# Seven-product weight pairs in 24 instead of 13 projection chunks of an encoder layer, with the attention work spread over the steps on two PSUM banks

## The chip, the cores and the metric

One core of one Trainium2 chip. The metric is the device time of one execution in microseconds (us), the median of three runs; one further execution was recorded by the hardware profiler, and all shares, rows and durations below are that execution's.

## The reference, cut to what matters

```python
h = layer_norm(x)                        # x: 256 tokens x 4096
p = h @ w_in                             # 4096 x 13312: 26 chunks of 512 columns
# attention, 16 query heads, 4 key/value heads of 128:
s = q @ k.T * 128**-0.5 - slope_h * |t - s|      (only |t - s| <= 128)
a = softmax over keys and one sink logit per head of s;  y_attn = (a @ v) * silu(z)
# convolution branch, 2048 channels:
y_conv = c_b * conv3(c_c * c_h) * silu(c_z)
out = layer_norm(2**0.25 * h + concat(y_conv, y_attn) @ w_out)
```

All of it is float32.

## The kernel before, in words

**A product of two floats as three.** TensorE reads float32 operands in a fast, rounded form (`F32R`). So each operand is cut into a rounded part `hi` and a rest `lo`, and x·w is taken as xh·wh + xh·wl + xl·wh, three matmuls into one PSUM accumulator. The normalised input stands transposed in `xT` (32 tiles of 128 rows, kt 0 to 31; hi of the 256 tokens, then lo). The weights come from HBM in steps, and each is cut in the kernel: `split_hi` (L124) has ScalarE (ACT) copy the raw tile into `whi`, `split_lo` (L129) has VectorE (DVE) subtract that from the raw tile into `wlo`.

**Steps and chunks.** The 13312 columns of the projection are 26 chunks of 512, in the order K, V, then Z and Q of each of four head groups, then for each of four channel groups CC, CH, CZ, CB (`IN_ORDER`, L36). A chunk takes all 32 tiles of kt. A plain step (`s`) brings four tiles of kt (1 MB) and multiplies with 24 matmuls of 512 columns (`mm`, L157). A pair step (`S`) brings two tiles of kt (0.5 MB) and forms the same 256 x 512 part of the product in Strassen's way, in seven products of half width (`mm_pair`, L176): 21 matmuls of 256 columns in place of 12 of 512. For it DVE makes four further blocks from the raw weights (`sums`, L112), the cut covers seven blocks, and sums of x stand in `SC` (`x_sums`, L499). Three of the seven products go into the chunk's accumulators `acc`, four into two banks `pacc`, which `pair_sums` (L513) and `whole` (L524) add in when the chunk is over. Before, 13 chunks have six pairs and five plain steps each (the first CZ to the last CZ); the other 13 chunks are eight plain steps.

**The order of the work is written by hand.** The main loop (L637) goes over the steps j. It issues the matmuls of step j, then whatever `at(j, ...)` has put down for that step, then the loads of step j+6 (or 7), then `sums(j + 4)` and `split(j + 3)`. Each engine works through its instructions in that order. `whi` and `wlo` have three buffers, so the cut for step j+3 begins when TensorE (PE) has finished step j, and has to be done before PE gets to step j+3: two steps later.

**A head group.** When chunk Q of a group is over, `q_turn` transposes q on PE. For each of its four heads come `scores` (6 matmuls on PE, then on DVE the bias, the row maximum and its negative `nm`, on ACT two exponentials with row sums and the sink's `es`, on DVE the denominator, its reciprocal `rd` and the division of the probabilities p), `p_tr` (four transposes on PE, `pT` cut into hi on ACT and lo on DVE), and `pv` (6 matmuls on PE, the gate on DVE). They stand at steps 2 to 8 after Q (L631), on four PSUM banks `att`.

Of the kernel before, what the change touches and what calls it, by code (L numbers as in the profile page):

```python
# [40 lines left out]
NS = 6  # L41
HW = W // 2
HT = S // 2
S_FIRST = IN_ORDER.index(C_CZ)
S_LAST = len(IN_ORDER) - 2
S_UNITS = "s S s S S s S s S S s".split()


def units(ci):

    if not S_FIRST <= ci <= S_LAST:
        return [("in", ci, q) for q in range(NPC)]
    q, p, us = 2 * NS // PK, 0, []
    for u in S_UNITS:
        if u == "s":
            us.append(("in", ci, q))
            q += 1
        else:
            us.append(("pair", ci, p))
            p += 1  # L60
    assert q == NPC and p == NS
    return us
# [9 lines left out]
def encoder_kernel(ctx: ExitStack, tc: tile.TileContext, x, emb_g, emb_b, wi, ws, conv_w, sink, wo, ln_g, ln_b, out):  # L72
# [25 lines left out]
    raw, wh, wl = {}, {}, {}  # L98

    def load(j, to=None):  # L100
        if j >= len(steps):
            return
        kind, a, b = steps[j]
        if kind == "pair":
            to = raw[j] = pc.tile([P, PIECE], F32, name="praw", bufs=3)
            nc.sync.dma_start(out=to[:, 0:4 * HW], in_=ws[IN_PAIRS.index((a, b))])
        else:
            if to is None:
                to = raw[j] = wpool.tile([P, PIECE], F32, name="wraw")
# [64 lines left out]
    pacc, SC = {}, None  # L174

    def mm_pair(j):  # L176

        _, ci, p = steps[j]
        hi, lo = (t.pop(j).rearrange("p (b w) -> p b w", w=HW) for t in (wh, wl))
        if p == 0:  # L180
# [3 lines left out]
        x = lambda kt, i: (xT[:, kt, i * HT:(i + 1) * HT], xT[:, kt, S + i * HT:S + (i + 1) * HT])  # L184
        sc = lambda k: (SC[:, p, 0, k, :], SC[:, p, 1, k, :])
        p0, p1, c0, c1 = pacc[ci, 0], pacc[ci, 1], acc[ci, 0], acc[ci, 1]
        for (ah, al), w, o, opens, closes in (
                (x(a, 0), 2, p0[:, 0, :], True, False), (x(b, 0), 3, c0[:, 0:HW], False, False),
                (sc(3), 1, c0[:, HW:W], False, False), (x(b, 1), 7, c1[:, 0:HW], False, False),
                (sc(0), 5, p1[:, 1, :], True, False), (sc(1), 6, p0[:, 1, :], False, True),  # L190
                (sc(2), 4, p1[:, 0, :], False, True)):
            nc.tensor.matmul(o, ah, hi[:, w, :], start=(opens and p == 0), stop=False)  # L192
            nc.tensor.matmul(o, ah, lo[:, w, :], start=False, stop=False)  # L193
            nc.tensor.matmul(o, al, hi[:, w, :], start=False, stop=(closes and p == NS - 1))  # L194
# [174 lines left out]
    ph = ExitStack()  # L369
    pa = ph.enter_context(tc.tile_pool(name="pa", bufs=1))  # L370

    def build_tab():
# [3 lines left out]
        tf = pa.tile([P, 2, S], F32, name="tf", tag="p", bufs=3)  # L376
# [42 lines left out]
    def end_z(ci, g):  # L419
        st_["z"] = token_tile(pa, "z", ci, AF.Silu)  # L420

    def z_turn(g):
        zT = st_["zT"] = pa.tile([P, GROUP, S], F32, name="zT")
        for b, ps in enumerate(turned(st_.pop("z"))):
            nc.scalar.activation(zT[:, 2 * b:2 * b + 2, :], ps, AF.Copy)
# [445 lines left out]
```

## Time and profile before

| | |
|---|---|
| median of three runs | 1561.48 us (1560.03 to 1562.35) |
| the profiled execution | 1562.12 us, span of its instructions 1560.3 us |
| granted TensorE clock, mean | 0.996 |
| busy DVE / ACT | 1056.4 us (68%) / 680.6 us (44%) |
| moved by DMA | 312.84 MB, 200 GB/s over the span |

The page of the profile gives the busy time of each engine, the chain of work that ended last, and the costliest groups of instructions. A group's row has line, engine, operation, output tile <- input tiles, shapes, the count, then the summed busy time and the mean of one in ns, then the idle time just before. In the timeline a row is one instruction or several alike: start, length, engine, line; square brackets hold the idle time before it and what ended it. PE rows overlap, since matmuls are pipelined: the distance between two starts is what one costs.

### The profile page before, as it was taken

Reading aid. Unit: us, or ns where it says so; the run is one execution under the profiler, and the core shown is the slowest. Engines: PE = TensorE matmul, PEld = TensorE weight load, DVE = VectorE, ACT = ScalarE, POOL = GpSimd, SP = SyncE. Lnnn points to the kernel's source line nnn. Section 1 sums busy time; section 2 is a strip of 40 time slices with the busy share of each in tenths; the row PEclk is TensorE's granted clock in tenths of the full one; section 3 lists DMA queues with packets and bytes.
Section 4 is the critical chain, followed back from the end, with each engine's and each line's share of the span. In section 5 each row is a group of like instructions: output and inputs, shape, how many; then the busy total and the mean of one; then the engine's idle time right before and its main releaser. Section 6 shows DMA issues by size and latency. Waiting matters only on the chain.

```text
span 1560.3 us, 18873 instructions
## 1 busy us (share of the span) xinstructions
PE 1541.5 (99%) x7884; PEld 1304.7 (84%) x7884; DVE 1056.4 (68%) x1072; ACT 680.6 (44%) x556; POOL 1.3 (0%) x7
## 2 busy tenths in 40 slices
PE   7999999999999999999999999999999999999997
PEld 4888888888888888888888888888888888888896
DVE  8644455464554678888888889888866665666656
ACT  4533345453453444544454445544555333333331
POOL 0000000000000000000000000000000000000000
PEclk9999999999999999999999999999999999999998
DMA  7555535545455455556555655656556666666662
GB/s 298 179 199 189 189 137 208 184 163 199 139 211 180 166 230 192 198 180 220 189 179 203 224 210 181 203 209 212 186 209 244 234 222 234 222 222 225 222 221 109
DMA packets 57589, 312.84 MB, mean 200 GB/s; under 512 B 6976, under 2 KB 8480, under 8 KB 27680
## 3 DMA queue, kind: packets, MB, share of 16 engines
q1 hardware_dynamic: 56928, 310.06, 55.7%
q8 instruction: 62, 1.02, 0.3%
q10 hardware_dynamic: 576, 1.57, 0.3%
q14 instruction: 23, 0.19, 0.0%
HBM read 303.66 MB, written 7.86 MB: 200 GB/s over the span
## 4 chain that ended last, share of the span: by engine, by line
PE 97%; DVE 1%; DMA 1%; ACT 0%; issue 0%; SPq 0%; DVEq 0%
PE acc L172 20%; PE acc L170 20%; PE acc L171 20%; PE acc L737 8%; PE acc L738 8%; PE acc L739 7%; PE pacc L194 2%; PE pacc L193 2%; PE pacc L192 2%; PE acc L194 2%; PE acc L193 2%; PE acc L192 2%; PE att L397 1%; DVE st L238 0%; DVE R L772 0%; PE acc L288 0%
## 5 line engine op out<-in xcount | busy, mean ns | idle before, releaser
L132 DVE TENSOR_TENSOR wlo<-wraw,whi 128x2048 fp32r<-128x2048 f32 x231 | 528.6, 2290 | 374.3 <-ACT whi L127 374.1
L127 ACT ACTIVATE whi<-wraw 128x2048 fp32r<-128x2048 f32 x231 | 441.8, 1914 | 497.3 <-PE acc L172 224.8
L172 PE MATMUL acc<-whi,xT 128*128 128x512 f32 x1336 | 525.2, 393 | 0.0
L170 PE MATMUL acc<-whi,xT 128*128 128x512 f32 x1336 | 524.8, 393 | 0.0
L171 PE MATMUL acc<-wlo,xT 128*128 128x512 f32 x1336 | 521.8, 391 | 0.0
L172 PEld LDWEIGHTS acc<-whi,xT 128*128 128x128 f32 x1336 | 251.0, 188 | 54.2
L171 PEld LDWEIGHTS acc<-wlo,xT 128*128 128x128 f32 x1336 | 250.9, 188 | 53.5
L170 PEld LDWEIGHTS acc<-whi,xT 128*128 128x128 f32 x1336 | 251.3, 188 | 50.0
L737 PE MATMUL acc<-whi,xT 128*128 128x512 f32 (+1 forms) x576 | 211.9, 368 | 0.0
L738 PE MATMUL acc<-wlo,xT 128*128 128x512 f32 (+1 forms) x576 | 211.5, 367 | 0.0
L739 PE MATMUL acc<-whi,xT 128*128 128x512 f32 (+1 forms) x576 | 210.2, 365 | 0.0
L127 ACT ACTIVATE whi<-praw 128x1792 fp32r<-128x1792 f32 x78 | 132.6, 1704 | 113.0 <-PE acc L172 65.7
L132 DVE TENSOR_TENSOR wlo<-praw,whi 128x1792 fp32r<-128x1792 f32 x78 | 157.2, 2023 | 17.3 <-ACT whi L127 16.5
L737 PEld LDWEIGHTS acc<-whi,xT 128*128 128x128 f32 x576 | 108.1, 188 | 19.6 <-issue 0.7
L739 PEld LDWEIGHTS acc<-whi,xT 128*128 128x128 f32 x576 | 108.1, 188 | 19.0
L738 PEld LDWEIGHTS acc<-wlo,xT 128*128 128x128 f32 x576 | 108.3, 188 | 17.4
L194 PE MATMUL pacc<-whi,SC 128*128 128x256 f32 x234 | 66.2, 283 | 0.0
L193 PE MATMUL pacc<-wlo,SC 128*128 128x256 f32 x234 | 66.2, 283 | 0.0
L192 PE MATMUL pacc<-whi,SC 128*128 128x256 f32 x234 | 66.2, 283 | 0.0
L117 DVE TENSOR_TENSOR praw<-praw 128x512 f32<-128x512 f32 x78 | 53.3, 684 | 0.0
L194 PEld LDWEIGHTS pacc<-whi,SC 128*128 128x128 f32 x234 | 44.9, 192 | 0.0
L193 PEld LDWEIGHTS pacc<-wlo,SC 128*128 128x128 f32 x234 | 44.6, 191 | 0.0
(169 smaller groups left out, 1143.6 us busy)
## 6 DMA issues: line engine op xcount, KB each, us to landing
wraw<-in_wi SPq DMA_DIRECT2D x167, 1024.0 KB, 4.9
wraw<-in_wo SPq DMA_DIRECT2D x64, 1024.0 KB, 4.9
praw<-in_ws SPq DMA_DIRECT2D x78, 512.0 KB, 4.1
yl<-yd SPq DMA_DIRECT2D x7, 512.0 KB, 5.7
xc<-in_x SPq DMA_DIRECT2D x14, 256.0 KB, 6.6
x<-in_x SPq DMA_DIRECT2D x6, 512.0 KB, 7.6
first<-in_wi SPq DMA_DIRECT2D x2, 1024.0 KB, 8.6
yd<-ya SPq DMA_DIRECT2D x4, 512.0 KB, 3.0
```

The lines of the kernel that those rows point to most:

```text
L117: nc.vector.tensor_tensor(r[:, 4:6, :], r[:, 1:3, :], r[:, 0:1, :].to_broadcast([P, 2, HW]), op=ALU.add)
L127: nc.scalar.activation(part(j, wh[j]), part(j, raw[j]), AF.Copy)
L132: nc.vector.tensor_tensor(part(j, wl[j]), part(j, raw.pop(j)), part(j, wh[j]).bitcast(F32), op=ALU.subtract)
L170: nc.tensor.matmul(a, xh, hk, start=(first and k == 0), stop=False)
L171: nc.tensor.matmul(a, xh, lk, start=False, stop=False)
L172: nc.tensor.matmul(a, xl, hk, start=False, stop=(last and k == PK - 1))
L192: nc.tensor.matmul(o, ah, hi[:, w, :], start=(opens and p == 0), stop=False)
L193: nc.tensor.matmul(o, ah, lo[:, w, :], start=False, stop=False)
L194: nc.tensor.matmul(o, al, hi[:, w, :], start=False, stop=(closes and p == NS - 1))
L737: nc.tensor.matmul(o, yh, hk, start=(s == 0), stop=False)
L738: nc.tensor.matmul(o, yh, lk, start=False, stop=False)
L739: nc.tensor.matmul(o, yl, hk, start=False, stop=(s == KT - 1))
```

## The change

1. **More pairs.** Each chunk has a number of pairs now (`PAIRS`): none in K and V, four in the next eleven (Z and Q of all groups, then the first CC, CH and CZ), six in the last thirteen (from the first CB to the last CB). The first CZ goes from six to four, the last CB from none to six, the eight Z and Q chunks and the first CC and CH from none to four. In all 122 pairs in place of 78.
2. **Sums of x early.** `x_sums` for the first four pairs runs in chunk V, for the other two in the first CZ. Of four sums of x that a pair needs, one now overwrites a block of `xT` and three stand in `SC`: four of the seven products read their stationary part from `xT`, three from `SC`.
3. **PSUM.** The two `pacc` banks are opened before the attention, which is left with two `att` banks in place of four.
4. **The attention is cut into smaller events** (`HEAD_STEPS`, `SPREAD`, `DENSE`): transposing q and its lo, scores, exponentials, normalising, transposing p and its lo, p·v, and gating are separate entries, at steps 1 to 17 after Q (to 15 for the last group). The division of p by its denominator goes from DVE to ACT (`norms`). The tiles `qhl` and `pT` have one buffer in place of two.
5. **The end of the projection.** The loads and cuts of y for the output projection are put down at steps of the last CB and the first output chunk. Every fourth raw weight tile goes to a further buffer (`wraw4`).

```diff
-S_UNITS = "s S s S S s S s S S s".split()
+PAIRS = [0, 0] + [4] * 11 + [6] * (len(IN_ORDER) - 13)
+N_SC = 4
+ORDERS = {0: "s" * 8, 4: "sSsSssSsSs", 6: "sSsSSsSsSSs"}
...
-                (sc(3), 1, c0[:, HW:W], False, False), (x(b, 1), 7, c1[:, 0:HW], False, False),
-                (sc(0), 5, p1[:, 1, :], True, False), (sc(1), 6, p0[:, 1, :], False, True),
-                (sc(2), 4, p1[:, 0, :], False, True)):
+                (sc(2), 1, c0[:, HW:W], False, False), (x(b, 1), 7, c1[:, 0:HW], False, False),
+                (sc(0), 5, p1[:, 1, :], True, False), (x(a, 1), 6, p0[:, 1, :], False, True),
+                (sc(1), 4, p1[:, 0, :], False, True)):
...
+    pps.close()
+    ps_att = pps.enter_context(tc.tile_pool(name="ps_att2", bufs=2, space=PSUM))
+    ps_p = pps.enter_context(tc.tile_pool(name="ps_p", bufs=2, space=PSUM))
...
     def end_q(ci, g):
-        st_["q"] = token_tile(pa, "q", ci, AF.Copy, P ** -0.5)
+        st_["q"] = whole_tile(pa, "q", ci, AF.Copy, P ** -0.5)
...
+    def exps(h):
         slope = 2.0 ** (-8.0 * (h + 1) / HEADS)
         s = pa.tile([P, 2, S], F32, name="s")
-        nc.vector.scalar_tensor_tensor(s, tab, slope, s_ps, op0=ALU.mult, op1=ALU.add)
+        nc.vector.scalar_tensor_tensor(s, tab, slope, st_.pop(("s", h)), op0=ALU.mult, op1=ALU.add)
...
+    def norms(h):
+        p, den, es = st_["p", h]
         nc.vector.tensor_tensor(den, den, es, op=ALU.add)
         rd = small.tile([P, 2], F32, name="rd")
         nc.vector.reciprocal(rd, den)
         for b in range(2):
-            nc.vector.tensor_scalar(p[:, b, :], p[:, b, :], rd[:, b:b + 1], None, op0=ALU.mult)
-        st_["p", h] = p
+            nc.scalar.activation(p[:, b, :], p[:, b, :], AF.Identity, scale=rd[:, b:b + 1])
...
+    HEAD_STEPS = [(1, q_tr, 0), (2, q_lo, 0), (3, scores, 0), (4, scores, 1), (4, exps, 0), (5, q_tr, 1), (5, exps, 1),
+                  (5, norms, 0), (6, p_tr, 0), (6, q_lo, 1), (6, norms, 1), (7, scores, 2), (7, p_lo, 0)]
+    SPREAD = [(8, pv, 0), (8, exps, 2), (9, p_tr, 1), (9, out_z, 0), (9, norms, 2), (10, scores, 3), (10, p_lo, 1),
+              (11, pv, 1), (11, exps, 3), (12, p_tr, 2), (12, out_z, 1), (12, norms, 3), (13, p_lo, 2), (14, pv, 2),
+              (14, p_tr, 3), (15, out_z, 2), (15, p_lo, 3), (16, pv, 3), (17, out_z, 3)]
+    DENSE = [(8, pv, 0), (8, p_tr, 1), (8, exps, 2), (9, scores, 3), (9, out_z, 0), (9, p_lo, 1), (9, norms, 2),
+             (10, pv, 1), (10, p_tr, 2), (10, exps, 3), (11, out_z, 1), (11, p_lo, 2), (11, norms, 3), (12, pv, 2),
+             (12, p_tr, 3), (13, out_z, 2), (13, p_lo, 3), (14, pv, 3), (15, out_z, 3)]
...
+        if fn is end_z:
+            at(j + 7, z_tr, 0)
+            at(j + 8, z_tr, 1)
+        if fn is end_q:
+            h = g * GROUP
+            for t, f, a in HEAD_STEPS + (SPREAD if g < NG - 1 else DENSE):
+                at(j + t, f, a if f in (q_tr, q_lo) else h + a)
```

How this moves instructions is shown at two places of the first head group. First, ACT from its first exponentials on, before (`p`, `den` and `es` are a head's exponentials and sums, `whi` the rounded part of a weight step, `pT` the transposed probabilities):

```order
L456 ACTIVATE p_1402,den_1403<-s_1396,nm_1400 128x256 x2
L457 ACTIVATE es_1404<-nm_1400,sk_87 128x2
L456 ACTIVATE p_1426,den_1427<-s_1420,nm_1424 128x256 x2
L457 ACTIVATE es_1428<-nm_1424,sk_87 128x2
L127 ACTIVATE whi_1439<-wraw_1278 128x2048
L456 ACTIVATE p_1480,den_1481<-s_1474,nm_1478 128x256 x2
L457 ACTIVATE es_1482<-nm_1478,sk_87 128x2
L127 ACTIVATE whi_1493<-wraw_1311 128x2048
```

and now, from the second head on, at steps 5 and 6 after Q (the three `whi` are those of steps 7, 8 and 9; 1792 columns are a pair's, 2048 a plain step's; L491 divides p):

```order
L137 ACTIVATE whi_1696<-wraw_1574 128x2048
L452 ACTIVATE qhl_1729<-att_1724 128x512
L481 ACTIVATE p_1737,den_1738<-s_1731,nm_1735 128x256 x2
L482 ACTIVATE es_1739<-nm_1735,sk_87 128x2
L491 ACTIVATE p_1685<-p_1685,rd_1744 128x256 x2
L137 ACTIVATE whi_1750<-wraw4_1605 128x1792
L500 ACTIVATE pT_1780<-att_1775 128x512
L491 ACTIVATE p_1737<-p_1737,rd_1784 128x256 x2
L137 ACTIVATE whi_1790<-wraw_1642 128x2048
```

The division stands on ACT now, behind the exponentials and ahead of the next step's `whi`; each of these needs a small result (`nm`, `rd`) of DVE first. Second, DVE between two weight steps of the same group, before:

```order
L132 TENSOR_TENSOR wlo_1495<-wraw_1311,whi_1493 128x2048
L402 TENSOR_TENSOR pT_1526<-att_1521,pT_1526 128x512
L402 TENSOR_TENSOR pT_1534<-att_1529,pT_1534 128x512
L447 SCALAR_TENSOR_TENSOR s_1544<-tab_508,att_1537 128x512
L449 TENSOR_REDUCE m_1546<-s_1544 128x2
L451 TENSOR_SCALAR nm_1548<-m_1546,sk_87 128x2
L458 TENSOR_TENSOR den_1551<-den_1551,es_1552 128x2
L460 RECIPROCAL rd_1557<-den_1551 128x2
L462 TENSOR_SCALAR p_1550<-p_1550,rd_1557 128x256 x2
L132 TENSOR_TENSOR wlo_1565<-wraw_1359,whi_1563 128x2048
```

and now, from `wlo` of step 8 to `wlo` of step 10 (L127 to L129 are the sums of a pair's weight blocks, here for step 11, L456 and L505 the lo of q and of `pT`):

```order
L142 TENSOR_TENSOR wlo_1752<-wraw4_1605,whi_1750 128x1792
L456 TENSOR_TENSOR qhl_1729<-att_1724,qhl_1729 128x512
L487 TENSOR_TENSOR den_1738<-den_1738,es_1739 128x2
L489 RECIPROCAL rd_1784<-den_1738 128x2
L142 TENSOR_TENSOR wlo_1792<-wraw_1642,whi_1790 128x2048
L505 TENSOR_TENSOR pT_1780<-att_1775,pT_1780 128x512
L127 TENSOR_TENSOR wraw_1748<-wraw_1748 128x512
L128 TENSOR_TENSOR wraw_1748<-wraw_1748 128x256
L129 TENSOR_TENSOR wraw_1748<-wraw_1748 128x256
L142 TENSOR_TENSOR wlo_1833<-wraw_1691,whi_1831 128x2048
```

The lo of `pT`, which p·v of the first head reads, stands behind `wlo` of step 9 now, and that behind ACT's second division.

More of the change, by code (lines that the diff above doesn't have):

```diff
@@ L590, in y_load @@
     def y_load(q):
[L591 removed]
+        if q < 3:
+            t = pc.tile([P, GROUP, S], F32, name="yl", tag="ug")
+        else:
+            t = pc.tile([P, GROUP, S], F32, name="yl", tag="praw", bufs=3)
+        st_["y", q] = t
         nc.sync.dma_start(out=t, in_=yd[q])
```

205 lines of the change are left out of this document (108 added, 97 removed).

## The prediction, made before the changed kernel was run

> **What bounds the kernel now.** First the page's busy times and its chain of work that ended last.
>
> ```profile
> PE 1541.5 (99%) x7884; PEld 1304.7 (84%) x7884; DVE 1056.4 (68%) x1072; ACT 680.6 (44%) x556; POOL 1.3 (0%) x7
> ...
> PE 97%; DVE 1%; DMA 1%; ACT 0%; issue 0%; SPq 0%; DVEq 0%
> ```
>
> PE is the bound: nearly the whole chain lies on it. Next the busy times in two stretches, one group of the attention (a Z and a Q chunk, 16 plain steps) and four chunks of the convolution branch with six pairs each. The columns are the length, then PE, weight loads, DVE, ACT and POOL, the granted clock, DMA share and GB/s.
>
> ```profile
> 260.03:357.32 97.29, 97.29 (x467) 81.20 (x465) 51.62 (x54) 43.93 (x50) 0.00 (x0) 1.00 0.51 178
> ...
> 779.50:950.28 170.78, 170.78 (x1002) 150.93 (x1001) 145.53 (x153) 82.61 (x53) 0.00 (x0) 1.00 0.56 200
> ```
>
> PE has no gap in either. So the time is the sum of PE's starts, as long as the cut weights come in time. With pairs DVE is busy for 145.5 of 170.8 us, without them for 51.6 of 97.3 us. The third view is PE's timeline at a pair step: the last plain matmul, the first of two pair steps, the first of the next plain step, and one 20 matmuls later.
>
> ```profile
> 902.75 0.39 PE L172 MATMUL acc<-whi,xT 128*128 128x512 f32 x1
> 902.98 0.28 PE L192 MATMUL pacc<-whi,xT 128*128 128x256 f32 x1
> ...
> 907.90 0.39 PE L170 MATMUL acc<-whi,xT 128*128 128x512 f32 x1
> ...
> 912.47 0.39 PE L172 MATMUL acc<-whi,xT 128*128 128x512 f32 x1
> ```
>
> Two pair steps took 907.90 - 902.98 = 4.92 us, 2.46 each. Twenty plain matmuls took 4.57 us, 0.2285 each, so a plain step is 24 x 0.2285 = 5.48 us and the half of it that a pair step replaces is 2.74 us.
>
> The fourth view is the timeline of DVE and ACT in the attention before, with the PE step that needs their last result.
>
> ```profile
> 227.40 0.51 ACT L456 ACTIVATE p<-s,nm 128x256 f32<-128x256 f32 x1 [3.94 <-DVE nm L451]
> ...
> 228.40 0.28 ACT L457 ACTIVATE es<-nm,sk 128x2 f32<-128x2 f32 x1
> 228.58 1.90 ACT L127 ACTIVATE whi<-wraw 128x2048 fp32r<-128x2048 f32 x1
> 230.39 1.06 ACT L401 ACTIVATE pT<-att 128x512 fp32r<-128x512 f32 x2
> ```
>
> ```profile
> 223.49 2.29 DVE L132 TENSOR_TENSOR wlo<-wraw,whi 128x2048 fp32r<-128x2048 f32 x1 [0.79 <-ACT whi L127]
> 225.70 0.68 DVE L447 SCALAR_TENSOR_TENSOR s<-tab,att 128x512 f32<-128x512 f32 x1
> 226.41 0.69 DVE L449 TENSOR_REDUCE m<-s 128x2 f32<-128x512 f32 x1
> 227.13 0.23 DVE L451 TENSOR_SCALAR nm<-m,sk 128x2 f32<-128x2 f32 x1
> 228.71 0.16 DVE L458 TENSOR_TENSOR den<-den,es 128x2 f32<-128x2 f32 x1 [1.35 <-ACT es L457]
> 228.91 0.17 DVE L460 RECIPROCAL rd<-den 128x2 f32<-128x2 f32 x1
> 229.11 0.62 DVE L462 TENSOR_SCALAR p<-p,rd 128x256 f32<-128x256 f32 x2
> 230.51 2.29 DVE L132 TENSOR_TENSOR wlo<-wraw,whi 128x2048 fp32r<-128x2048 f32 x1 [0.79 <-ACT whi L127]
> ...
> 238.74 2.29 DVE L132 TENSOR_TENSOR wlo<-wraw,whi 128x2048 fp32r<-128x2048 f32 x1 [0.79 <-ACT whi L127]
> ```
>
> ```profile
> 241.86 0.48 PE L170 MATMUL acc<-whi,xT 128*128 128x512 f32 x1
> ```
>
> The two engines wait for each other in turn: DVE makes `nm`, ACT the exponentials (227.40 to 228.68), DVE the reciprocal and the division, and only then does ACT come to `whi` and DVE to `wlo`. The last `wlo` shown ends at 241.03. It is that of step 7 after Q, and PE begins that step at 241.86. So with all steps 5.48 us long and four heads' chains inside, 0.8 us are left of the slack. The change shortens two steps in five to 2.46 us here and lengthens this chain; that is where I look.
>
> **The change part by part.** *Pairs.* 122 in place of 78 are 44 more, each 2.74 - 2.46 = 0.28 us less of PE: 44 x 0.282 = 12.4 us. The product that now reads `xT` may go faster as well:
>
> ```profile
> 903.32 0.28 PE L192 MATMUL acc<-whi,xT 128*128 128x256 f32 x1
> ...
> 903.66 0.28 PE L192 MATMUL acc<-whi,SC 128*128 128x256 f32 x1
> ...
> 904.02 0.28 PE L192 MATMUL acc<-whi,xT 128*128 128x256 f32 x1
> ```
>
> Three matmuls from `xT` took 0.34 us, three from `SC` 0.36. If the place is the reason, all 122 pairs gain 0.02 us, 2.4 in all; if the weights' block is, nothing. I take 1.3. The gain on PE is 13.7 us, with ends 12.4 and 14.8.
>
> *The attention's chain.* These are the means of the instructions on it, one row for each kind:
>
> ```profile
> L132 DVE TENSOR_TENSOR wlo<-praw,whi 128x1792 fp32r<-128x1792 f32 x78 | 157.2, 2023 | 17.3 <-ACT whi L127 16.5
> L127 ACT ACTIVATE whi<-praw 128x1792 fp32r<-128x1792 f32 x78 | 132.6, 1704 | 113.0 <-PE acc L172 65.7 <-PE pacc L194 22.4 <-DVE praw L119 21.2
> ...
> L117 DVE TENSOR_TENSOR praw<-praw 128x512 f32<-128x512 f32 x78 | 53.3, 684 | 0.0
> ...
> L118 DVE TENSOR_TENSOR praw<-praw 128x256 f32<-128x256 f32 x78 | 33.2, 425 | 2.7
> ...
> L402 DVE TENSOR_TENSOR pT<-att,pT 128x512 fp32r<-128x512 f32 x16 | 10.6, 682 | 0.0
> ...
> L564 ACT ACTIVATE t<-att,cw 128x256 f32<-128x256 f32 x16 | 6.7, 472 | 17.8 <-PE att L397 17.8
> ...
> L484 DVE TENSOR_TENSOR ya<-att,zT 128x256 f32<-128x256 f32 x16 | 6.7, 422 | 15.0 <-PE att L481 15.0
> ...
> L520 DVE TENSOR_TENSOR e<-pacc,e 128x256 f32<-128x256 f32 x13 | 5.5, 425 | 1.7 <-PE acc L172 0.5
> ...
> L527 DVE TENSOR_TENSOR sz<-acc,e 128x512 f32<-128x512 f32 x8 | 5.1, 682 | 0.0
> ...
> L517 ACT ACTIVATE e<-pacc 128x256 f32<-128x256 f32 x13 | 4.7, 364 | 0.0
> ...
> L401 ACT ACTIVATE qhl<-att 128x512 fp32r<-128x512 f32 x8 | 4.3, 596 | 14.1 <-PE att L397 14.1
> ...
> L536 ACT ACTIVATE sz<-sz 128x1024 f32<-128x1024 f32 x4 | 4.2, 1062 | 15.1 <-DVE sz L527 15.1
> ```
>
> In the timeline above, independent work on one engine starts about 0.08 us before the row ahead ends (223.49 + 2.29 against 225.70), and the other engine about 0.03 us after it (227.36 to 227.40). A plain `wlo` then counts 2.21 us inside a run, a pair's 1.94, the three sums 1.52 (0.72, 0.46, 0.34), a head's exponentials 1.67 on DVE and 1.19 on ACT. For the division on ACT no row stands; the nearest is L564, a scaled copy of the same shape, 0.47 us each, and its bounds are DVE's 0.35 and the exponential's 0.5. Two make 0.77.
>
> Now I walk from the copy of the second q (`q_tr` 1, step 5). Steps 6 to 13 after Q are S s S s s S s S. The clock starts with ACT's copy, 0.25 us after PE has transposed.
>
> ACT: copy 0.49, exponentials of head 1 1.19, division of head 0 0.77, `whi` of step 8 1.71, so 4.2 us. DVE: its `wlo` 1.97, q's lo 0.60, denominator and reciprocal 0.38: 7.1. ACT: division of head 1 0.79, `whi` of step 9 1.92: 9.8. DVE: `wlo` 9 2.24, lo of `pT` 0.60, sums for step 11 1.52, `wlo` 10 2.21, exponentials of head 2 1.67: 18.1. ACT: its part 1.22, `whi` 11 1.71: 21.0. DVE: `wlo` 11 1.97, gate 0.34, reciprocal 0.38: 23.7. ACT: division 0.79, copy of `pacc` 0.36, as the Z chunk has just ended: 24.8. DVE: `pair_sums` 1.80, sums for step 13 1.52, `wlo` 12 2.21, lo of `pT` 0.60, `whole` 1.28: 32.2. ACT: Silu 1.00, `whi` 13 1.71: 35.0. DVE: `wlo` 13 1.97, exponentials of head 3 1.67: 38.6. ACT: 1.22 and `whi` 14 1.92: 41.7. DVE: `wlo` 14, 2.3: 44.0 us.
>
> PE's own work in that stretch is four plain steps (21.9) and four pair steps (9.8), and seven of a group's 16 attention events. A group's 97.29 us less 16 x 5.48 leaves 9.55 us for all 16, so 4.2 for these. PE would reach step 14 at 35.9 - 0.25 = 35.7 us and finds its weights at 44.0 plus 0.2 to start: 8.5 us late. Parts of this show earlier, since p·v needs the lo of `pT` and its bank: 0.4 us at p_tr of head 0, about 1.2 at pv of head 0 (lo ready at 12.7), 3.0 at pv of head 1 (lo ready at 31.0), the rest as a wait of some 3.6 us ahead of step 14. After it pv of head 2 waits another 0.8, because its lo stands behind `wlo` 15. That makes 9.3 us in each of three groups. After step 15 only little stands between the weight steps and the lag is made up.
>
> The last group uses `DENSE`. There the second transpose stands ahead of the exponentials of head 2 on the same step, and needs the bank that these set free, at 17.1 us on the same clock: PE waits 3.6 us. Walked in the same way, its waits are 0.4, 1.2, 3.6, 0.7 (scores 3 behind the gate of head 0), 1.4 (p_tr 2 behind the exponentials of head 3) and 0.6: 8.0 us. Together 3 x 9.3 + 8.0 = 35.9 us.
>
> *The rest at nothing.* `x_sums` add at most 3.5 us of DVE each, by the nearest wider rows (a L402, four L118, two more lo's). In V a plain step leaves DVE 5.48 - 2.29 = 3.2 us, so four of them overrun by 1.2 us at most, and two steps of slack hide that. A chunk with six pairs has DVE busy for 145.5 / 4 = 36.4 of 42.7 us; two `x_sums` in the first CZ, or three cuts of y in the last CB, make about 40. If that cover fails, I allow 3 us in all, in the range. Loads have a tile more in the attention, and 178 GB/s over 97.3 us become about 166 over 104.
>
> **A rule weighed.** A rule on the clock would make the waits cost more. The trace shows what a gap does at the kernel's end, by the granted clock in the column after POOL:
>
> ```profile
> 1545.00:1550.00 5.00, 1.81 (x13) 1.31 (x11) 3.65 (x15) 0.29 (x1) 0.00 (x0) 0.94 0.55 210
> 1550.00:1560.00 10.00, 4.39 (x8) 2.27 (x8) 5.36 (x8) 0.27 (x1) 0.00 (x0) 0.50 0.53 210
> ```
>
> With PE idle for 3.2 of 5 us the clock fell from full to half. No gap of 3 us inside dense work is in the trace. The Trainium skill, page "TensorE: Matmul & The Clock Gate", section "HAM oscillation — how this bites in real kernels", says that a gap in PE's work above about 3.4 us brings the clock to half. By that rule the waits of 3.0 and 3.6 us lie just about at the limit; the rows at the end agree with it, and it is the third rival below.
>
> **The sum.** 1562.1 (the profiled execution) - 13.7 + 35.9 = 1584.3 us. The median of the runs is 0.6 us lower: 1583.7, so 1584.
>
> **The rivals.** *No waits (it goes faster).* ACT and DVE keep up and PE stays without a gap: 1562.1 - 13.7 - 0.6, so 1548 us. For it speaks that before, DVE is idle for 47% of a group and that steps with pairs ran without a gap at 85% of DVE. Against it: there the cut never waited for exponentials, and in the walk DVE is idle for some 18 of 44 us because it waits for ACT. The place that decides is `norms` ahead of `whi` on ACT at steps 5 and 6; under 3.4 us of waits a group (13.7 / 4) the kernel is faster. Chance 0.14. *Half the waits.* The divisions and exponentials overlap better than the rows let me assume, 4.5 us a group: 1548 + 18, so 1566 us. Chance 0.12. *The waits cost clock.* Each of about seven waits of 3 us or more (two a group, one in the last) leaves PE at the half clock of the last window. If a whole pair step then runs at half speed, that is 2.46 us more each, 17 in all; if a half of one, 9. Between them 1584 + 12 = 1596 us. Chance 0.12. The forecast keeps 0.62.
>
> **How the numbers follow.** About 0.2% is what a measurement of this kernel can tell from no change, 3.1 us. The forecast and the clock rival are slower, 0.74; of the half case 0.08 are slower, 0.03 within 0.2% and 0.01 faster; of the no-wait case 0.13 are faster and 0.01 within 0.2%. That gives slower 0.82, same 0.04, faster 0.14. The range leaves out the no-wait case and little else. Its lower end lets the waits be 6 us a group at the larger gain: 1561.5 - 14.8 + 24 = 1571, and reaches towards the half case, 1567. Its upper end takes in the clock rival: 1597.
>
> **What would show it.** In the profile after, a group of the middle (transposes of z to transposes of z) should last 95.0 us of PE plus about 9 of waits, 104 us against 97.29; PE should wait for `pT` by DVE's lo, and for `wlo`. DVE should wait for `whi` right after the exponentials and divisions. Pair steps should take 2.44 to 2.46 us. A group of 95 us without waits of PE would prove the walk wrong, at the handoffs between ACT and DVE; a clock below 0.95 in the attention's windows would be the third rival.

## The result and the profile after

| | before | after |
|---|---|---|
| median of the runs | 1561.67 us (4 runs, 1560.03 to 1562.35) | 1587.99 us (4 runs, 1586.86 to 1590.03) |
| the profiled execution | 1562.12 us, span 1560.3 us | 1590.03 us, span 1588.2 us |
| granted clock, mean | 0.996 | 0.991 |

The ratio is 1.0172, with a 95% interval of 1.0154 to 1.0189: 26 us slower. The profiled execution lies 2 us above the median.

First the page: busy times and shares of the chain. DVE and ACT stand in it now.

```profile
PE 1542.4 (97%) x8280; PEld 1318.9 (83%) x8280; DVE 1176.7 (74%) x1281; ACT 724.8 (46%) x613; POOL 1.3 (0%) x7
...
PE 85%; DVE 9%; ACT 4%; issue 1%; DMA 1%; SPq 0%; DVEq 0%; ACTq 0%
```

PE's busy time is the same as before (1541.5) though its work is less; the reason comes below. PE's waits, from the view of waits (line, what ended the wait, us in total, times, longest):

```profile
PE att L512 <- DVE pT L505: 12.3, 7, 2.7
...
PE acc L181 <- DVE wlo L142: 6.2, 5, 1.8
PE att L498 <- DVE s L472: 4.0, 2, 3.4
...
PE acc L180 <- ACT whi L137: 1.9, 2, 1.0
PE att L416 <- DVE g L590: 1.9, 1, 1.9
```

L512 is p·v, L498 the transposing of p, L180 and L181 the first two matmuls of a plain step, L416 in the last row the transposing of `g` at the end of the last CB. None of these waits was there before. Next the windows of the first and the third of three head groups (transposes of z to transposes of z), then of two convolution chunks:

```profile
190.50:296.55 106.05, 99.43 (x539) 85.19 (x537) 72.92 (x87) 54.41 (x63) 0.00 (x0) 0.97 0.44 161
...
402.53:508.00 105.47, 99.26 (x550) 85.49 (x548) 72.56 (x86) 53.95 (x64) 0.00 (x0) 0.98 0.48 168
808.49:893.65 85.16, 85.16 (x502) 75.23 (x501) 73.82 (x80) 42.48 (x29) 0.00 (x0) 1.00 0.54 199
```

A group takes 106 us instead of 97.3. Of these PE is idle for 6.6 (106.05 - 99.43). Two convolution chunks with twelve pairs take 85.16 us, against 85.39 before:

```profile
779.34:864.73 85.39, 85.39 (x502) 75.46 (x501) 73.94 (x80) 42.45 (x29) 0.00 (x0) 1.00 0.56 197
```

So the product that reads `xT` did get faster, by 0.23 / 12 = 0.019 us a pair.

Now the chain of the walk in the first group. ACT, from its copy of the second q, with the idle time in brackets:

```profile
228.72 0.60 ACT L452 ACTIVATE qhl<-att 128x512 fp32r<-128x512 f32 x1 [4.35 <-PE att L416]
...
235.89 0.91 ACT L491 ACTIVATE p<-p,rd 128x256 f32<-128x256 f32 x2 [2.54 <-DVE rd L489]
236.70 3.70 ACT L137 ACTIVATE whi<-wraw 128x2048 fp32r<-128x2048 f32 x2
246.92 0.51 ACT L481 ACTIVATE p<-s,nm 128x256 f32<-128x256 f32 x1 [6.52 <-DVE nm L476]
...
248.11 1.69 ACT L137 ACTIVATE whi<-wraw 128x1792 fp32r<-128x1792 f32 x1
```

and DVE in the same stretch:

```profile
232.90 2.03 DVE L142 TENSOR_TENSOR wlo<-wraw,whi 128x1792 fp32r<-128x1792 f32 x1 [4.37 <-ACT whi L137]
...
238.63 2.29 DVE L142 TENSOR_TENSOR wlo<-wraw,whi 128x2048 fp32r<-128x2048 f32 x1 [2.84 <-ACT whi L137]
...
249.82 2.03 DVE L142 TENSOR_TENSOR wlo<-wraw,whi 128x1792 fp32r<-128x1792 f32 x1 [3.00 <-ACT whi L137]
...
270.54 2.29 DVE L142 TENSOR_TENSOR wlo<-wraw,whi 128x2048 fp32r<-128x2048 f32 x1 [3.15 <-ACT whi L137]
```

ACT sits idle for 6.52 us ahead of an exponential that needs `nm`, while the `whi` behind it could have been made; then DVE sits idle for 3.00 us because that `whi` is late. Each engine waits in turn with work queued behind the wait. The last row is the `wlo` of step 14. PE's waits from p·v of head 0 up to that step, and the matmuls around the last:

```profile
241.67 0.36 PE L512 MATMUL att<-pT,v 128*128 128x256 f32 x1 [1.08 <-DVE pT L505]
...
259.92 0.39 PE L512 MATMUL att<-pT,v 128*128 128x256 f32 x1 [2.66 <-DVE pT L505]
...
269.33 0.28 PE L207 MATMUL pacc<-whi,SC 128*128 128x256 f32 x1
270.56 0.50 PE L180 MATMUL acc<-whi,xT 128*128 128x512 f32 x1 [0.95 <-ACT whi L137]
272.88 0.80 PE L181 MATMUL acc<-wlo,xT 128*128 128x512 f32 x1 [1.83 <-DVE wlo L142]
273.48 0.63 PE L182 MATMUL acc<-whi,xT 128*128 128x512 f32 x1
273.90 0.63 PE L180 MATMUL acc<-whi,xT 128*128 128x512 f32 x1
```

Behind the gap two starts lie 0.42 us apart (273.48 to 273.90), in place of 0.23. That is half clock, and it counts as busy. The windows around it have the granted clock behind POOL's column, 0.51 for six microseconds:

```profile
262.00:269.00 7.00, 6.94 (x42) 5.80 (x41) 3.54 (x4) 4.61 (x9) 0.00 (x0) 1.00 0.28 94
269.00:273.00 4.00, 1.22 (x8) 0.71 (x6) 2.46 (x2) 1.99 (x2) 0.00 (x0) 0.89 0.24 100
273.00:279.00 6.00, 6.00 (x15) 4.69 (x16) 4.57 (x8) 4.30 (x4) 0.00 (x0) 0.51 0.27 87
279.00:285.00 6.00, 6.00 (x33) 5.10 (x32) 3.64 (x6) 2.40 (x2) 0.00 (x0) 1.00 0.89 332
```

The second group goes the same way. In the third the wait ahead of p·v of head 1 is again 2.66 us, but there it brings half clock (0.62 over the next stretch, in the first group 1.00 behind the same wait). Step 14 then waits 1.77 us and runs at full clock, and p·v of head 2 waits 0.66 us for the lo of `pT`:

```profile
471.95 0.39 PE L512 MATMUL att<-pT,v 128*128 128x256 f32 x1 [2.66 <-DVE pT L505]
...
491.25 0.38 PE L513 MATMUL att<-pT,v 128*128 128x256 f32 x1 [0.66 <-DVE pT L505]
```

```profile
473.00:477.50 4.50, 4.50 (x14) 3.54 (x13) 1.79 (x2) 3.93 (x3) 0.00 (x0) 0.62 0.22 86
```

### The profile page after: what moved, and what is told of

The parts are those of the page before. It is cut to its first block, busy times and chain, and to the rows that moved or that the text cites. A ratio compares the mean times of both kernels' runs of the same rounds, so it can differ in the third digit from the quotient of the medians.

```text
span 1588.2 us, 20011 instructions
## 1 busy us (share of the span) xinstructions
PE 1542.4 (97%) x8280; PEld 1318.9 (83%) x8280; DVE 1176.7 (74%) x1281; ACT 724.8 (46%) x613; POOL 1.3 (0%) x7
## 4 chain that ended last, share of the span: by engine, by line
PE 85%; DVE 9%; ACT 4%; issue 1%; DMA 1%; SPq 0%; DVEq 0%; ACTq 0%
PE acc L181 15%; PE acc L182 15%; PE acc L180 15%; PE acc L785 7%; PE acc L787 7%; PE acc L786 7%; DVE wlo L142 4%; PE pacc L207 3%; PE pacc L205 3%; PE pacc L206 3%; PE acc L207 2%; PE acc L206 2%; PE acc L205 2%; ACT whi L137 2%; PE att L416 1%
## 5 line engine op out<-in xcount | busy, mean ns | idle before, releaser
L142 DVE TENSOR_TENSOR wlo<-wraw,whi 128x2048 fp32r<-128x2048 f32 (+1 forms) x250 | 560.9, 2245 | 324.4 <-ACT whi L137 312.6
L137 ACT ACTIVATE whi<-wraw 128x2048 fp32r<-128x2048 f32 (+1 forms) x250 | 468.6, 1879 | 431.1 <-PE acc L787 190.9
L181 PE MATMUL acc<-wlo,xT 128*128 128x512 f32 x1160 | 458.1, 395 | 6.2 <-DVE wlo L142 6.2
L180 PE MATMUL acc<-whi,xT 128*128 128x512 f32 x1160 | 458.7, 395 | 1.9 <-ACT whi L137 1.9
L182 PE MATMUL acc<-whi,xT 128*128 128x512 f32 x1160 | 459.3, 396 | 0.0
L181 PEld LDWEIGHTS acc<-wlo,xT 128*128 128x128 f32 x1160 | 219.9, 190 | 54.3 <-DVE wlo L142 8.5
L182 PEld LDWEIGHTS acc<-whi,xT 128*128 128x128 f32 x1160 | 220.1, 190 | 46.6
L180 PEld LDWEIGHTS acc<-whi,xT 128*128 128x128 f32 x1160 | 220.3, 190 | 46.0 <-ACT whi L137 2.3
L142 DVE TENSOR_TENSOR wlo<-praw,whi 128x1792 fp32r<-128x1792 f32 x81 | 163.2, 2022 | 18.5 <-ACT whi L137 16.5
L787 PEld LDWEIGHTS acc<-whi,xT 128*128 128x128 f32 x576 | 108.0, 188 | 19.6
L786 PEld LDWEIGHTS acc<-wlo,xT 128*128 128x128 f32 x576 | 108.1, 188 | 18.9
L785 PEld LDWEIGHTS acc<-whi,xT 128*128 128x128 f32 x576 | 108.3, 188 | 17.5 <-issue 0.7
L205 PE MATMUL pacc<-whi,xT 128*128 128x256 f32 x244 | 69.5, 285 | 0.0
L205 PE MATMUL pacc<-whi,SC 128*128 128x256 f32 x244 | 69.0, 283 | 0.0
L207 PE MATMUL pacc<-whi,SC 128*128 128x256 f32 x244 | 68.9, 282 | 0.0
L207 PE MATMUL acc<-whi,xT 128*128 128x256 f32 x244 | 68.0, 279 | 0.0
L207 PE MATMUL pacc<-whi,xT 128*128 128x256 f32 x244 | 67.9, 278 | 0.0
```

The costliest lines, as they stand in the source:

```text
L137: nc.scalar.activation(part(j, wh[j]), part(j, raw[j]), AF.Copy)
L142: nc.vector.tensor_tensor(part(j, wl[j]), part(j, raw.pop(j)), part(j, wh[j]).bitcast(F32), op=ALU.subtract)
L180: nc.tensor.matmul(a, xh, hk, start=(first and k == 0), stop=False)
L181: nc.tensor.matmul(a, xh, lk, start=False, stop=False)
L182: nc.tensor.matmul(a, xl, hk, start=False, stop=(last and k == PK - 1))
L785: nc.tensor.matmul(o, yh, hk, start=(s == 0), stop=False)
```

## The experiments

The theory at the start was the walk's: ACT and DVE hand the work to and fro (head events ahead of `whi` on ACT), and the shorter pair steps leave them too little time. The rivals were that the two PSUM banks or the small events make the waits by themselves, that DVE's load in pair steps does, or that half clock is the main cost. Ratios are those to the kernel before, with 95% intervals. Its median beside the runs was 1561.92 to 1562.24 us.

### The division back on DVE

```diff
-            nc.scalar.activation(p[:, b, :], p[:, b, :], AF.Identity, scale=rd[:, b:b + 1])
+            nc.vector.tensor_scalar(p[:, b, :], p[:, b, :], rd[:, b:b + 1], None, op0=ALU.mult)
```

> The changed kernel with the division of p put back on DVE; events, banks and pairs as they are. Handoff theory (ACT and DVE wait for each other, and the division stands on ACT ahead of the next whi): walking a group as before without the division on ACT, the waits fall from 11 us a group to about 5 (pv of head 1 one us, step 14 still 3.5 us with its half clock), so 1588 - 14 to 20, about 1571. Rival banks (two att banks and single buffers make PE wait): nothing moves, 1588. Rival DVE work (DVE simply has too much to do with pairs): DVE gets 16 x 0.6 us more, so 1588 or slower.

1573.88 us, ratio 1.0077 (1.0060 to 1.0094), near the 1571 of the handoff theory. The first group:

```profile
190.88:291.83 100.95, 97.73 (x538) 84.15 (x537) 75.15 (x95) 51.23 (x55) 0.00 (x0) 0.98 0.47 170
```

DVE has more to do (75.15 us in place of 72.92) and the group is 5.1 us shorter, so DVE's load isn't what makes PE wait. Taking this one handoff out of the chain, with the rest of the order as it is, gives back 14 us.

### whi first in every step

In the main loop `split_hi(j + 3)` is issued right behind the matmuls, ahead of all events of the step; `split_lo` stays at its end.

```diff
         mm_pair(j) if kind == "pair" else mm(j)
+        split_hi(j + 3)
         for fn, a in later.pop(j, []):
...
-        split(j + 3)
+        split_lo(j + 3)
```

> The changed kernel with only the order on ACT altered: whi of step j+3 is issued ahead of the events of step j, wlo stays behind them. No work, bank or buffer changes. Handoff theory: DVE no longer waits for whi after each exponential or division; left are about 1.5 us at the first transposition of p (its division now stands behind a whi) and 0.9 at pv of head 1, no gap of 3 us and no half clock: 1548 + 10, about 1558. Rival banks: 1588, the banks are freed by the same instructions. Rival DVE work: 1588, since DVE does the same work.

1586.74 us, ratio 1.0168 (1.0146 to 1.0190): the expectation failed. The view of waits shows a new one in each group, and two convolution chunks took 86.00 us where the change takes 85.16:

```profile
PE att L416 <- ACT q L576: 9.0, 4, 2.2
```

```profile
717.91:803.91 86.00, 85.59 (x502) 75.24 (x501) 71.37 (x75) 40.79 (x26) 0.00 (x0) 1.00 0.58 212
```

`whi` of step j+3 waits until PE is through with step j, since it takes over that step's buffer. All that stands behind it on ACT waits too: here the copy out of `pacc`, Silu and q's scale, and q is needed by PE at the very next step. The edit had moved two kinds of events at once, so its time told nothing of the head events alone. ACT's waits for `nm`, 40.1 us in the change, were down to 3.0.

### The lo matmuls last in a step

In `mm` the 16 matmuls with `whi` come first, then the 8 with `wlo`.

```diff
                 nc.tensor.matmul(a, xh, hk, start=(first and k == 0), stop=False)
-                nc.tensor.matmul(a, xh, lk, start=False, stop=False)
-                nc.tensor.matmul(a, xl, hk, start=False, stop=(last and k == PK - 1))
+                nc.tensor.matmul(a, xl, hk, start=False, stop=False)
+        for k in range(PK):
+            for i in range(2):
...
+                nc.tensor.matmul(acc[ci, i], xT[:, kt, i * P:(i + 1) * P], lo[:, k * W:(k + 1) * W], start=False,
+                                 stop=(last and k == PK - 1))
```

> The changed kernel, in a plain step the 16 matmuls that need only whi come first and the 8 with wlo last. The gap of 3.5 us ahead of step 14 then shrinks to about 1.3 (only whi is waited for), without the half clock behind it. Handoff theory: pv of head 2 after that step still waits for the lo of pT, which DVE has only at the end of the same chain, so what is saved is just what the half clock put behind that point, 1.8 us a group: 1588 - 6, about 1582. Rival clock (the half clock is what makes the kernel slower than the walk of the waits alone, 2.7 us each): 1588 - 10 or more, 1578 or less. If the cut weights alone were the limit and not the chain behind them: 1588 - 4 x 5 = 1568.

1589.52 us, ratio 1.0178 (1.0163 to 1.0193): no gain, where the handoff theory had expected 1582. PE has no wait ahead of step 14 now, and the wait stands one event later, ahead of p·v of head 2:

```profile
260.28 0.58 PE L516 MATMUL att<-pT,v 128*128 128x256 f32 x1 [2.67 <-DVE pT L509]
279.58 0.39 PE L517 MATMUL att<-pT,v 128*128 128x256 f32 x1 [2.77 <-DVE pT L509]
```

This fits a chain on DVE and ACT that sets when the group goes on, while PE's order only moves the wait. The run doesn't price half clock, since it didn't go: the mean clock is 0.990, and behind the first of the two waits it is 0.52 up to 263.30, where the change has 1.00 behind the same wait.

### Both: division on DVE and whi first

The first two edits together.

> Division on DVE and whi first together. Handoff theory: nearly all waits gone, at most about 1 us a group (pv of head 1): 1548 to 1552, faster than the kernel before by 10 to 14 us, and conv stage and pairs as in the changed kernel. Rival banks and rival DVE work: 1580 or slower, DVE has 10 us more to do and PE the same two banks.

1576.69 us, ratio 1.0096 (1.0081 to 1.0111). It failed in its total for the same reason as `whi` first: q's scale (9.2 us of waits in four groups) and slower convolution chunks. But the first group took 97.7 us (transposes of z at 190.6 and 288.3), 8.4 less than in the change, with the wait for q (2.2 to 2.5 us) still in it.

### No pairs in the attention chunks

`PAIRS` is 0 for Z and Q (90 pairs stay), all groups use `DENSE`, and the early `x_sums` come in the last Q chunk (the expectation calls it the second-last).

```diff
-PAIRS = [0, 0] + [4] * 11 + [6] * (len(IN_ORDER) - 13)
+PAIRS = [0] * 10 + [4] * 3 + [6] * (len(IN_ORDER) - 13)
...
-            for t, f, a in HEAD_STEPS + (SPREAD if g < NG - 1 else DENSE):
+            for t, f, a in HEAD_STEPS + DENSE:
```

> Only the pairs of the ten chunks K, V, Z and Q are taken out (90 pairs in all, in CC, CH, CZ and CB), the sums of x are made in the second-last Q chunk and all four groups use DENSE; the two att banks, the new events and the division on ACT stay. If the chain of ACT and DVE makes the waits because two steps in five are 3 us shorter (my theory), eight plain steps leave it time: PE without waits over 1 us in the attention, 1562 - 12 x 0.28 - 2 = 1556 to 1558 us. If two banks or the cut into events make the waits (rival), they stay: 1570 or more. If the gap at half clock is what costs, it goes with the gap, so this run doesn't tell it apart.

1586.91 us, ratio 1.0163 (1.0148 to 1.0178). The theory said 1556 to 1558, so it failed as it stood. The waits for `wlo` and `pT` were gone, as it said, and another had come, in all four groups:

```profile
PE att L465 <- DVE ya L519: 13.6, 4, 3.9
```

Scores of head 3 need the bank that p·v of head 0 holds until DVE has gated it (`ya`). So shorter steps are not needed for PE to wait. Either two banks or the late DVE was the cause; the runs under "Plain attention chunks" below take that up.

### whi ahead of the head events only

Events of a chunk's end stay ahead of `whi`; the head events and the turning of z come behind it. The division goes back to DVE as well.

```diff
+        evs = later.pop(j, [])
+        for fn, a in evs:
+            if fn not in HEAD_FNS:
+                fn(*a)
+        split_hi(j + 3)
+        for fn, a in evs:
+            if fn in HEAD_FNS:
+                fn(*a)
...
-        split(j + 3)
+        split_lo(j + 3)
```

> The division of p is back on DVE, and whi of step j+3 stands on ACT ahead of the attention's head events and of the turning of z, but behind the events of a chunk's end (the two runs before had it ahead of these too, and q's scale then made PE wait 2.5 us a group). All 122 pairs stay. My theory: the waits for wlo and pT are those of the run with both edits (3 to 6 us in all), the 9 us of waits for q and the 5.5 us in the convolution chunks go: 1577 - 9 - 5.5 - 3 for fewer episodes at half clock, so about 1557 to 1562 us, at or a little under the kernel before. Rival (it is DVE's load in pair steps, no order helps): 1572 or more, as with the division alone.

1553.48 us, ratio 0.9956 (0.9938 to 0.9973): faster than both kernels, and 4 us better than expected. The first group; the other two of the middle take the same 95.18 us:

```profile
190.93:286.11 95.18, 95.18 (x537) 83.05 (x536) 75.09 (x96) 51.59 (x55) 0.00 (x0) 1.00 0.49 178
```

PE has no gap and full clock, with DVE and ACT about as busy as in the change (75.1 and 51.6 us against 72.9 and 54.4). In the timeline of ACT `whi` comes ahead of the exponentials, which find their `nm` ready:

```profile
222.69 1.92 ACT L137 ACTIVATE whi<-wraw 128x2048 fp32r<-128x2048 f32 x1 [4.51 <-PE acc L182]
...
228.92 1.70 ACT L137 ACTIVATE whi<-wraw 128x1792 fp32r<-128x1792 f32 x1 [1.71 <-issue]
...
231.00 0.50 ACT L481 ACTIVATE p<-s,nm 128x256 f32<-128x256 f32 x1
```

ACT's waits for `nm` over the whole kernel fell from 40.1 us at 10 places to 3.8 at 6. The division's waits for `rd`, 31.3 us in the change, left ACT together with the division. The change, then this run:

```profile
ACT p L481 <- DVE nm L476: 40.1, 10, 6.5
ACT p L491 <- DVE rd L489: 31.3, 12, 3.4
```

```profile
ACT p L481 <- DVE nm L476: 3.8, 6, 1.0
```

### The same order, the division on ACT

> The same order as in the run with whi ahead of the head events, but the division of p stays on ACT as in the change. My theory: order and division each take a part of the waits; 1587 - 9 (waits for q) - 5.5 (convolution chunks) - 3 = about 1568 us, between the run with both and the change. Rival (the order of whi is worth nothing, the first try with it showed 1587): 1584 to 1588.

1558.60 us, ratio 0.9981 (0.9972 to 0.9990), better than expected. The order alone is worth 1588.0 - 1558.6 = 29.4 us, more than the 26.3 that the change had lost. On which engine the division is done is worth 5 us then, not 14. PE waits here for what it doesn't wait for there: 3.8 us in four groups for p, whose division on ACT stands behind `whi` now.

### Only the exponentials behind whi

The set of events behind `whi` is cut to `exps`; the division on ACT, the copies of q and of `pT` stay ahead of it.

```diff
-    HEAD_FNS = {z_tr} | {f for _, f, _ in HEAD_STEPS + SPREAD + DENSE}
+    HEAD_FNS = {exps}
```

> The change with one edit: only the exponentials (with the bias, maximum and nm on DVE that they need) stand behind whi of step j+3 in the same step; the division on ACT, the copies of q and pT and all else stay ahead of it. If each head event ahead of whi has its share of the lag (division and exponentials about half each, as the run without the division on ACT showed 14 of 29 us), 1570 to 1575 us. If the exponentials' wait for nm is the whole matter, about 1559 us, as with all head events behind whi. If the division is (its place decides, as the prediction said), over 1580 us.

1562.13 us, ratio 1.0001 (0.9991 to 1.0011), nearest to the second case. Moving this one event gives back 26 us, moving the others 3.5 more. Such shares don't add up: taking the division off ACT in the old order gave back 14. The division's waits for `rd` fell as well, from 31.3 us to 13.8, though it kept its place ahead of `whi`. The edit also puts the reciprocal of head 0 ahead of the exponentials of head 1 on DVE at step 5; what that is worth by itself isn't shown. A group takes 96.74 us:

```profile
190.67:287.41 96.74, 95.95 (x538) 83.05 (x537) 72.83 (x88) 54.78 (x63) 0.00 (x0) 1.00 0.48 177
```

### Plain attention chunks: order or banks

First the run without pairs in the attention, with `whi` ahead of the head events (the edit of the order as above, the division on ACT):

> The run with plain attention chunks, with one edit: whi of step j+3 stands on ACT ahead of the head events. Plain attention alone lost its waits for wlo and pT but got a new one, scores of head 3 behind the gate of head 0 (13.6 us in four groups), since only two banks are there. If the gate comes late because DVE waits for whi behind the exponentials (order theory), the wait shrinks to under 1.5 us a group and the time to 1558 to 1568 us. If two banks force it in whatever order (bank theory), it stays over 3 us a group and the time over 1580 us.

1562.01 us, ratio 1.0001 (0.9991 to 1.0011), as the order theory expected. The wait for the gate is down from 13.6 to 1.0 us, and a group takes what it took before the change, 97.29:

```profile
195.27:292.53 97.26, 97.26 (x466) 81.06 (x464) 48.69 (x46) 48.50 (x59) 0.00 (x0) 1.00 0.49 175
```

Then the old order with four `att` banks until the attention is over:

```diff
-PAIRS = [0] * 10 + [4] * 3 + [6] * (len(IN_ORDER) - 13)
+PAIRS = [0] * 12 + [4] + [6] * (len(IN_ORDER) - 13)
...
+            if ci == c_ch0:
+                open_banks()
```

> The run with plain attention chunks, with four att banks until the attention is over (the two pacc banks open after the first CH, so the first CC and CH are plain too: 82 pairs); whi stays behind the head events. Bank theory: without pairs and with four banks nothing of the change is left that makes PE wait, so no waits over 1 us and 1562 - 4 x 0.28 - 1.5 = about 1559 us. Order theory: the late gate no longer holds a bank, so the 13.6 us go here too, and what is left shows as waits for pT or wlo: up to 1568 us. If the cutting into small events costs by itself, 1575 us or more.

1564.52 us, ratio 1.0012 (1.0002 to 1.0021), and once more with the end of the first CC one step earlier:

> The run with plain attention chunks and four att banks once more, with the end of the first CC one step earlier, ahead of the first CZ, whose first step takes over its accumulators (the first try read them one step too late, so its first channel group was computed from wrong sums; the work was the same). The same 1564 to 1566 us as the first try, with PE's waits in the attention under 2 us each.

1564.71 us, ratio 1.0012 (1.0002 to 1.0022). In both runs the first CC and CH multiply by `xT` after `x_sums` has overwritten one block in each of the first four pairs' tiles, so the first channel group differs from the reference, with the same amount of work; the reason that the second expectation gives for this is not the one. PE's waits for the gate are gone here too; the only one left in the attention is 0.8 us, for the lo of `pT`. ACT still waits in the second run, 33.4 us for `rd` and 19.4 for `nm`, so with plain steps and four banks these waits cost PE next to nothing. So two banks and the late DVE make the wait together: either more banks or the better order takes it away. Neither is a bound by itself in plain attention chunks; pairs with four banks were not tried.

### Gaps of known size in the kernel before

DVE writes `wlo` over itself ahead of six plain steps, so that PE has one gap at each.

```diff
+GAP = {13: 9152, 20: 8064, 28: 9920, 44: 7296, 60: 8576, 76: 11264}
...
+        while n > 0:
+            m = min(n, PIECE)
+            nc.vector.tensor_tensor(wl[j][:, 0:m], wl[j][:, 0:m].bitcast(F32), wl[j][:, 0:m].bitcast(F32), op=ALU.max)
+            n -= m
```

> The kernel before, with DVE kept busy for longer ahead of six plain steps (13, 20, 28, 44, 60, 76) by writing wlo over itself, so that PE has one gap of a known size at each, about 3.2, 2.0, 4.0, 1.2, 2.6 and 5.5 us by the slack of two plain steps. If a gap of about 3 us brings half clock (third rival's mechanism), the windows behind the gaps of 3.2, 4.0 and 5.5 us show a clock of 0.5 for some 6 us and their matmuls a pitch of 0.43 us, and the others show 1.00. If half clock in the change has another cause (its many small matmuls), all six stay at 1.00. Span 1560 + 18.5 of gaps + 3 x 2.7 = 1587 or 1579 us.

1591.21 us in one run. The six gaps were 1.53, 2.29, 3.05, 3.61, 4.41 and 6.06 us long. Here are the second and the third of these, with the matmuls behind them:

```profile
143.04 0.51 PE L177 MATMUL acc<-wlo,xT 128*128 128x512 f32 x1 [2.29 <-DVE wlo L137]
143.38 0.40 PE L178 MATMUL acc<-whi,xT 128*128 128x512 f32 x1
...
393.82 0.79 PE L177 MATMUL acc<-wlo,xT 128*128 128x512 f32 x1 [3.05 <-DVE wlo L137]
394.41 0.63 PE L178 MATMUL acc<-whi,xT 128*128 128x512 f32 x1
394.84 0.63 PE L176 MATMUL acc<-whi,xT 128*128 128x512 f32 x1
...
397.31 0.40 PE L176 MATMUL acc<-whi,xT 128*128 128x512 f32 x1
```

After the gap of 2.29 us the matmuls run on as ever, after the one of 3.05 they start 0.43 us apart until 397.31, 3.5 us after the gap. The gap of 1.53 is as the former, the three longer ones as the latter. So a gap of PE alone, without any of the change's events, brings half clock, for 3 to 4 us and not the 6 that were expected.

The length of a gap alone doesn't decide it, as the other runs show. Of three gaps of 3.23 us in the run with plain attention chunks, the first left full clock, the other two brought half. With `whi` first a gap of only 2.24 us brought it, and in the run of both edits one of 3.19 us did not. These two, each with the window behind it:

```profile
210.15 0.68 PE L416 MATMUL att<-ident,q 128*128 128x128 f32 x4 [2.24 <-ACT q L576]
```

```profile
210.15:214.10 3.95, 3.95 (x13) 3.17 (x14) 2.96 (x2) 2.23 (x2) 0.00 (x0) 0.57 0.58 198
```

```profile
1213.73 1.09 PE L416 MATMUL att<-ident,g 128*128 128x128 f32 x8 [3.19 <-DVE g L590]
```

```profile
1214.00:1218.00 4.00, 4.00 (x23) 3.42 (x22) 2.44 (x2) 1.66 (x2) 0.00 (x0) 1.00 0.60 213
```

## Why the prediction was right or wrong

*The direction and the size.* Forecast 1584 us and slower, measured 1588, inside the range and slower by 1.7%. The profiled execution was to be 1584.3 and was 1590.0. The direction and the mechanism (ACT and DVE late for PE) were right; the sum came out for reasons that are luck in part, as the terms show. The run with `whi` ahead of the head events and the division on DVE has the change's PE work and few waits, so the terms are set against it.

*The walk.* It said 44.0 us from ACT's copy of the second q to the end of `wlo` of step 14. The rows give 270.54 + 2.29 - 228.72 = 44.1. The waits ahead of p·v were to be 1.2 and 3.0 us; the trace has 1.08 and 2.66. The wait ahead of step 14 was to be 3.6 (by the walk's own terms 8.5 - 4.6 = 3.9, and its 9.3 takes that); the rows give 0.95 + 1.83 = 2.8. The wait of 0.4 at p_tr of head 0 isn't in the trace. The wait of 3.6 us in the last group, ahead of the second transposing of p, was 3.4. So the order of the queues and the rows of before were enough to work out the chain on ACT and DVE; what PE waits for it came out too long. One reading is off: in the walk's terms DVE waits for ACT for 16.8 of the 44 us, not some 18.

*The group.* Forecast 95.0 of PE and 9.3 of waits. The run with the better order shows PE's work as 95.18. The change took 106.05, 10.9 more: 6.6 as idle time of PE where 9.3 were forecast, and 99.43 - 95.18 = 4.25 as matmuls that went slower, about 3 of it at half clock. The last group has 131.0 us from its transposes of z to the first of u (508.0 to 639.0) against 126.0 (476.5 to 602.5), 5.0 where 8.0 were forecast. In all 317.5 - 285.5 = 32.0 in the three groups and 5.0 are 37 us, forecast 35.9 (the run that this is set against has 1.1 us of wait itself). The sum is nearly right, but its make-up isn't: about 23.5 us are idle time of PE, 13.5 slow matmuls. That 12 us too many of waits met 13.5 us of slow matmuls, which the sum had at nothing, is luck. Some 9 of the 13.5 are half clock; that is an estimate from the granted clock, 0.53, 0.52, 0.62 and 0.57 over 6.4, 6.1, 4.5 and 3.8 us of PE's work behind the four gaps concerned. Where the rest comes from is open.

*Half clock.* The third rival's mechanism took place, once in every group, alongside the forecast: in the first two ahead of step 14, in the third behind p·v of head 1, in the last behind the wait of 3.4 us. The rival had counted seven waits, and its price of 12 us for them (9 to 17) meets the 9 that the four took only at its low end. It doesn't come on top of 35.9 either, since idle time was only 23.5. The sentence "No gap of 3 us inside dense work is in the trace" was the gap in my evidence. The rule of the Trainium skill, page "TensorE: Matmul & The Clock Gate", section "HAM oscillation — how this bites in real kernels", puts the limit at about 3.4 us. The runs agree that a gap brings half clock, but not on the limit: 2.24 us was enough once, and 3.19 was not once. The wait of 0.8 us forecast at p·v of head 2 is in the trace in the third group only, with 0.66 us, where step 14 ran at full clock; in the first two PE came there at half clock, later than the lo of `pT` was ready.

*The pairs' gain.* Forecast 13.7 us. The run without waits in the groups has 1562.1 - 1553.2 = 8.9 in the profiled executions. The product from `xT` gave 0.019 x 122 = 2.3, more than the 1.3 taken, so 14.7 were to be had. What is short lies outside the middle groups for the most part: in that run PE still waits 1.1 us for a bank in the last group and 1.6 us for `g` at the end of the last CB, which did not wait before. Waits for `wlo` in the first CZ, where two `x_sums` stand, are another 0.8. Of the remaining 2.3 us the three middle groups have 0.9, with 95.18 us each where 97.29 - 8 x 0.301 = 94.88 were to be had; the rest I can't place. "The rest at nothing" was wrong in the two places that it named, the first CZ and the last CB, by 2.4 us together. The pairs' gain, short by 4.8 us of the forecast, is most of what took the sum too low.

*The place that decides.* The prediction put it at "`norms` ahead of `whi` on ACT at steps 5 and 6". That step failed. The exponentials ahead of `whi` decide: moved behind it alone, they give back 26 us, and the division with all other head events another 3.5. The division isn't without weight in the old order, where taking it off ACT gave back 14 us: both stand in one chain. The walk itself had the reason in it, the places at which ACT waits for `nm`, but I named the instruction that was new and not the one that waited longest (6.52 us).

*The reason of the shorter steps.* The walk explains the waits by pair steps of 2.46 us. The runs without pairs show that this is one of two ways: with plain steps of 5.48 us PE waits as well, for a bank, when only two are there. What is common to the slow versions that keep the old order is a DVE that runs late because ACT stands still ahead of `whi`. The kernel before had this order too, with 0.8 us of slack; which of its four banks, its lumped events and its longer steps gave it these was not tried one by one.

## What to carry to other kernels

Where two engines feed a third through queues that are worked off in order, look at what stands ahead of the feeding instruction: anything that waits for the other engine (here the exponentials for `nm`) should come behind it, and anything that the third engine needs at the next step should stay ahead of it, since the feeding instruction itself waits for a buffer. A hand-made walk along two queues, with durations from the trace of before, gave the end of their chain to 0.1 us (the waits of PE less well, 9.3 us a group against 6.6), so it is worth doing for the order without the suspect as well. A gap of PE of two to three microseconds can cost clock on top of its length.

## What the runs showed of the hardware that I had not expected

- Single gaps of PE shorter than expected brought half clock for 3 to 4 us: one of 3.05 us in dense plain matmuls, one of 2.24 us with `whi` first. One of 2.29 us in dense matmuls and one of 3.19 us in the run of both edits did not, and the same wait of 2.66 us in the change did in the third group and not in the first two. In the first group of the change, where the gap ahead of step 14 had one matmul in its middle (0.95 and 1.83 us of waits), half clock lasted 6 us. Why one gap does and another doesn't stays open.
- Matmuls of 256 columns that read their stationary part from `xT` instead of `SC` took less: 0.019 us for the three of a pair's product. It is the moved product that gained: from its first start to the next product's, 0.360 us before and 0.3415 now (means of 48 pairs each, from the timelines of PE).
